# Two chunks' inner products in one visit of the matrix engine, and four copies of each sample token

## The chip, the core and the metric

The kernel runs on one core of a Trainium2 chip. The metric is the device time of one execution in microseconds: before the change 1611.52 us, the median of three runs (1607.17 to 1611.88 us). A core has the matrix engine TensorE (PE; its weight loads are listed as PEld), VectorE (DVE), ScalarE (ACT), GpSimd (POOL) and SyncE (SP), which here issues the transfers (DMAs). PE writes into PSUM, eight banks of 512 float32 numbers per partition. Each engine works through its own queue in order and waits at semaphores for the others.

## The reference

Two layers stand one behind the other in a residual trunk: a pooling mixer and a Mamba-2 state-space (SSD) mixer. They run over a prompt of 1024 tokens and over 8 sample sequences of 8 tokens with carried states. The part that matters here, cut to its core:

```python
# x: tokens x heads x 64;  B, C: tokens x groups x 128;  chunks of 128 tokens
a_cum = cumsum(dt * A, within the chunk)
L  = exp(where(causal, a_cum[i] - a_cum[j], -inf))
y_diag = einsum((C_i . B_j) * L[i, j] * dt[j], x[j])              # inside the chunk
state  = einsum(B[j], exp(a_cum[end] - a_cum[j]) * dt[j], x[j])   # what the chunk adds
h_next = exp(a_cum[end]) * h + state                              # from chunk to chunk
y_off  = einsum(C[i], h, exp(a_cum[i]))                           # from the incoming state
y = y_diag + y_off
```

The samples use the same formulas with chunks of 8 tokens. All is float32.

## The kernel before

Features lie on the partitions. The kernel works through two halves (h = 0, 1); each holds 512 prompt tokens and four sample sequences of 8 tokens (32 columns), so T = 544. Each projection is made by `product` (L166) in three float32r passes (high part by high, high by low, low by high), two halves of 272 columns each. `layer0` is the pooling mixer of one half, `layer1` the SSD mixer. The low parts of the SSD weights are made ahead by `stash` (L133 to L137), in buffers named L and bA, and stored.

`layer1` runs over four groups of heads; a group has two quads of four heads. `ssd` handles the prompt tokens of a quad, in four chunks of 128 tokens. For a chunk it loads the cumulated decays (bA), masks them on POOL (L624), takes the exponentials on ACT (L628) and multiplies by the C.B products on DVE (L629), which gives L. PE transposes x (L632), DVE scales it into xd and xs (L636). Four products xd by L (L639), each 64 columns of the array wide, go into the bank dg. The incoming state gives two products (L648) into the bank `of`, which DVE multiplies by the decays bE (L649) and to which it adds dg (L651). The product L655 gives what the chunk adds to the state; POOL decays the old state (L660) and DVE adds (L661). In half 0 the first chunk has no incoming state and its dg is copied by ACT (L653).

`ssd_sample` does the same for the 32 sample tokens of a quad. What they add to the state is made by one float32r product per sequence (L724) over 96 rows: three copies of each token (high part, low part and high part of B against high, high and low part of x).

The program's order is not written by hand: a scheduler lays out each engine's queue from the code and its priorities, so that the many large products L166 of projections stand between the small products of `ssd`. A change of buffers or of code order lays out all queues anew.

Of the kernel before, what the change touches and what calls it, by code (L numbers as in the profile page):

```python
# [9 lines left out]
F32 = mybir.dt.float32  # L10
F32R = mybir.dt.float32r
AF = mybir.ActivationFunctionType
ALU = mybir.AluOpType
# [3 lines left out]
P = 128  # L17
# [4 lines left out]
NH = 32  # L22
HD = 64
NS = 128
LP = 512
NB = 4
LS = 8
SM = NB * LS
# [9 lines left out]
Q = 128  # L38
NCH = LP // Q
# [6 lines left out]
C_ROW = C_SMASK + SM  # L46
# [16 lines left out]
def constants():  # L63
    c = np.zeros((P, C_END), np.float32)
    c[:, C_ID:C_ID + 128] = np.eye(128)
    j, i = np.meshgrid(np.arange(SM), np.arange(SM), indexing="ij")
    m = (j <= i) & (j // LS == i // LS)
    for r in range(3):
        c[r * SM:(r + 1) * SM, C_SMASK:C_SMASK + SM] = m
        for b in range(NB):  # L70
            c[r * SM + b * LS:r * SM + (b + 1) * LS, C_ROW + b] = 1.0
    c[:, C_INV:C_INV + 16] = np.float32(1.0) / np.arange(1, 17, dtype=np.float32)
    return c
# [3 lines left out]
def pool_ssd_step(ctx, tc, xin, spool, sconv, sssm, w_pin, w_mix, w_pout, w_sin, w_dt, w_sout, params, consts,  # L77
                  y_out, pool_p, pool_s, conv_p, conv_s, ssm_p, ssm_s):
    nc = tc.nc
    V, S, G, PE = nc.vector, nc.scalar, nc.gpsimd, nc.tensor  # L80
# [48 lines left out]

    def stash(n):  # L130
        for k, src, a, b in todo[:n]:
            raw = sp.tile([P, 512], F32, name="L", bufs=3)[:, :b - a]
            nc.sync.dma_start(out=raw, in_=src[:, a:b])  # L133
            hl = sp.tile([P, 512], F32R, name="bA", bufs=2)[:, :b - a]
            S.copy(hl, raw)  # L135
            V.tensor_tensor(out=hl, in0=raw, in1=hl, op=ALU.subtract)  # L136
            nc.sync.dma_start(out=low[k][:, a:b], in_=hl.bitcast(F32))  # L137
        del todo[:n]
# [324 lines left out]
    acd = [dp.tile([NCH, NH, Q], F32, name=f"acd{h}") for h in range(2)]  # L463
# [8 lines left out]
    def dt_part(h, act):  # L472
# [62 lines left out]
            nc.sync.dma_start(out=d2[:, k], in_=d1[h][k].rearrange("(b h) l -> h b l", b=NB))  # L535
        nc.sync.dma_start(out=asd[h], in_=d2[:, 0].rearrange("h b l -> h (b l)"))
        nc.sync.dma_start(out=esd[h], in_=d2[:, 3].rearrange("h b l -> h (b l)"))
        d3 = sp.tile([NH, 3, 3, SM], F32, name="cd")
        for k in range(3):
            G.tensor_copy(out=d3[:, k], in_=d2[:, k:k + 1].rearrange("h k b l -> h k (b l)").broadcast_to([NH, 3, SM]))  # L540
        sat = sp.tile([3 * SM, 3, NH], F32, name="sat")
        pt = sps.tile([P, 3, NH], F32, name="tr", bufs=2)
        for k in range(3):
            PE.transpose(pt[:3 * SM, k], d3[:, k].rearrange("p r s -> p (r s)"), ident[:NH, :NH])
        S.mul(sat[:, 0], pt[:3 * SM, 0], -1.0)
        S.copy(sat[:, 1:], pt[:3 * SM, 1:])
        return nat, sat, cdb

    def conv_part(h, act, g, j):
# [51 lines left out]
    def heads(x):  # L601
        return x.rearrange("p (e d) -> p e d", e=4)
# [4 lines left out]
    def by_head(x, i):  # L607

        return x[:, i:i + 4, None].broadcast_to([x.shape[0], 4, HD])

    def ssd(h, g, q, x, ys, C, com, nat, cdb):
        h0 = g * 8 + q * 4
        hf = None
        if h == 1:
            hf = sp.tile([P, 2 * P], F32, name=f"hf{q}", bufs=2)
            nc.sync.dma_start(out=hf, in_=hsd[g, q])
        for c in range(NCH):
            cs = slice(c * Q, (c + 1) * Q)
            ci = c * NH + h0
            bs, bt = com[c]  # L620

            bA = sp.tile([P, 4, Q], F32, name="bA", bufs=2)
            nc.sync.dma_start(out=bA, in_=acd[h][c:c + 1, h0:h0 + 4].broadcast_to([P, 4, Q]))
            G.affine_select(out=bA, in_=bA, pattern=[[0, 4], [1, Q]], compare_op=ALU.is_ge, fill=-1e30, base=0,  # L624
                            channel_multiplier=-1)
            L = sp.tile([P, 4, Q], F32, name="L", bufs=3)
            for e in range(4):
                S.activation(out=L[:, e], in_=bA[:, e], func=AF.Exp, bias=nat[:, 0, ci + e:ci + e + 1])  # L628
            V.tensor_tensor(out=L, in0=L, in1=bs.broadcast_to([P, 4, Q]), op=ALU.mult)  # L629
            px = sps.tile([P, 2 * P], F32, name="tr", bufs=2)  # L630
            for k in range(2):
                PE.transpose(px[:, k * P:(k + 1) * P], x[:, k, cs], ident)  # L632
            xd = sp.tile([P, 2 * P], F32, name="xd", bufs=2)
            xs = sp.tile([P, 2 * P], F32, name="xs", bufs=2)
            for k, x1 in enumerate((xd, xs)):
                V.tensor_tensor(out=heads(x1), in0=heads(px), in1=by_head(nat[:, 1 + k], ci), op=ALU.mult)  # L636
            pd = sps.tile([P, 2, Q], F32, name="dg")
            for e in range(4):
                PE.matmul(pd[e % 2 * HD:(e % 2 + 1) * HD, e // 2], xd[:, e * HD:(e + 1) * HD], L[:, e], start=True,  # L639
                          stop=True)  # L640
            if hf is not None:
                bE = sp.tile([P, 2, Q], F32, name="bE", bufs=2)
                ev = ecd[h][c:c + 1, h0:h0 + 4].rearrange("c (k r) i -> c r k i", r=2)
                for r in range(2):
                    nc.sync.dma_start(out=bE[r * 64:(r + 1) * 64], in_=ev[:, r].broadcast_to([64, 2, Q]))
                po = sps.tile([P, 2, Q], F32, name="of")
                for k in range(2):
                    PE.matmul(po[:, k], hf[:, k * P:(k + 1) * P], C[:, cs], start=True, stop=True)  # L648
                V.tensor_tensor(out=ys[:, :, cs], in0=po, in1=bE, op=ALU.mult)  # L649
            if hf is not None:  # L650
                V.tensor_tensor(out=ys[:, :, cs], in0=ys[:, :, cs], in1=pd, op=ALU.add)  # L651
            else:
                S.copy(ys[:, :, cs], pd)  # L653
            pst = sps.tile([P, 2 * P], F32, name="stt")
            PE.matmul(pst, bt, xs, start=True, stop=True)  # L655
            hn = sp.tile([P, 2 * P], F32, name=f"hf{q}", bufs=2)
            if hf is None:
                S.copy(hn, pst)
            else:
                G.tensor_tensor(out=heads(hn), in0=heads(hf), in1=by_head(cdb, ci), op=ALU.mult)  # L660
                V.tensor_tensor(out=hn, in0=hn, in1=pst, op=ALU.add)  # L661
            hf = hn
        nc.sync.dma_start(out=ssm_p[g, q] if h == 1 else hsd[g, q], in_=hf)

    K3 = 3 * SM

    def sample_common(B, C):
        ss = slice(LP, T)

        bd = sp.tile([P, 3, SM], F32R, name="bd")  # L670
        S.copy(bd[:, 0], B[:, ss])
        V.tensor_tensor(out=bd[:, 1], in0=B[:, ss], in1=bd[:, 0], op=ALU.subtract)
        S.copy(bd[:, 2], B[:, ss])
        pb = sps.tile([P, NS], F32R, name="tr", bufs=2)
        PE.transpose(pb[:K3], bd.rearrange("p r s -> p (r s)"), idr)
        Bm = sp.tile([K3, NB, NS], F32R, name="Bm")
        for b in range(NB):
            V.tensor_scalar(out=Bm[:, b], in0=pb[:K3], scalar1=cst[:K3, C_ROW + b:C_ROW + b + 1], scalar2=None,
                            op0=ALU.mult)
        pS = sps.tile([P, SM], F32, name="tr", bufs=2)  # L680
        PE.matmul(pS[:SM], B[:, ss], C[:, ss], start=True, stop=True)
        Sm = sp.tile([SM, 1, SM], F32, name="Ss")
        V.tensor_tensor(out=Sm[:, 0], in0=pS[:SM], in1=cst[:SM, C_SMASK:C_SMASK + SM], op=ALU.mult)
        return Bm, Sm

    def ssd_sample(h, g, q, x, ys, C, com, sat, cdb):
# [11 lines left out]
        xr = sp.tile([P, 2, 3, SM], F32, name="xr")  # L698
        V.tensor_copy(out=xr, in_=x[:, :, None, ss].broadcast_to([P, 2, 3, SM]))
        for k in range(2):  # L700
            PE.transpose(px[:K3, k * P:(k + 1) * P], xr[:, k].rearrange("p r s -> p (r s)"), ident)
# [3 lines left out]
        V.tensor_tensor(out=heads(xs[:K3]), in0=heads(px[:K3]), in1=by_head(sat[:, 2], h0), op=ALU.mult)  # L705
        xh = sp.tile([K3, 2 * P], F32R, name="xh", bufs=2)
        S.copy(xh, xs[:K3])
        r2 = slice(2 * SM, 3 * SM)
        V.tensor_tensor(out=xh[r2], in0=xs[r2], in1=xh[r2], op=ALU.subtract)
        pd = sps.tile([P, 2, SM], F32, name="dg")  # L710
        for e in range(4):
# [305 lines left out]
```

## Time and profile before

| what | us |
|---|---|
| median of three runs | 1611.52 |
| the profiled execution | 1614.12 |
| its span, first to last instruction | 1612.3 |
| PE busy (modelled), of the span | 1571.3 |
| DVE busy | 1086.4 |
| ACT busy | 740.6 |
| POOL busy | 325.7 |
| mean granted clock of PE, of full speed | 0.992 |

PE's records overlap: a product is recorded from its start until its result is out, so the distance between starts tells what it costs the queue. A float32 product is recorded as two matrix instructions, one of float32r as one. Busy shares are of the profiled execution, which lies 2.6 us above the median.

### The profile page before, as it was taken

To read this page: it belongs to the slowest core of one execution; us is meant where nothing else is said; L and a number is where in the kernel's file an instruction comes from. 1 tells how busy PE (TensorE), PEld (TensorE's weight loads), DVE (VectorE), ACT (ScalarE), POOL (GpSimd) and SP (SyncE) were. 2 spreads that over 40 slices of the span, in tenths; PEclk is the share of its full clock that TensorE was granted. 3 is DMA by queue.
4 is the path that set the end of the run, shared out by engine and by line. 5 is a ranking of instruction groups with operands and counts; after the bars stand their busy time and mean duration, and the time that the engine had idled before them with its cause. 6 is when DMAs were issued, how large, how long until landed. Compare 5 with 4: busy or idle time off the path is not lost.

```text
span 1612.3 us, 33214 instructions
## 1 busy us (share of the span) xinstructions
PE 1571.3 (97%) x12644; PEld 1515.7 (94%) x12644; DVE 1086.4 (67%) x2108; ACT 740.6 (46%) x1454; POOL 325.7 (20%) x536
## 2 busy tenths in 40 slices
PE   9989999999999999999999999999999999999996
PEld 8989999999999999999898999989988999999995
DVE  7787878875446475668575476667768765765666
ACT  5554444554232324265555454543634645535432
POOL 1200000003100010023413113222326432131213
PEclk9999999999999999999999999999999999999998
DMA  8878788886323234465756656665666666575662
GB/s 288 295 241 281 252 283 273 298 260 210 100 84 98 93 91 123 134 196 154 231 165 211 196 174 201 202 209 183 205 204 194 215 194 212 174 215 181 190 229 93
DMA packets 163407, 315.82 MB, mean 196 GB/s; under 512 B 33072, under 2 KB 71600, under 8 KB 163248
## 3 DMA queue, kind: packets, MB, share of 16 engines
q1 hardware_dynamic: 163248, 313.70, 61.1%
q8 instruction: 99, 1.62, 0.4%
q14 instruction: 60, 0.49, 0.1%
HBM read 262.47 MB, written 51.16 MB: 195 GB/s over the span
## 4 chain that ended last, share of the span: by engine, by line
PE 81%; DMA 8%; DVE 5%; ACT 2%; issue 2%; POOL 1%; SPq 0%; DVEq 0%; ACTq 0%; POOLq 0%
PE big L166 70%; DMA low<-bA 4%; PE dg L639 2%; PE stt L655 2%; PE of L648 2%; DMA bA<-acd 1%; DMA bAs<-asd 1%; PE tr L632 1%; DMA sq<-x2d 1%; DVE bA L136 1%; DMA L<-in_w_sin_dram 1%; PE big L386 1%; PE stt L724 1%; PE of L720 1%; DVE wlo L151 1%
## 5 line engine op out<-in xcount | busy, mean ns | idle before, releaser
L166 PE MATMUL big<-ah,whi 128*128 128x272 f32 (+1 forms) x2304 | 668.6, 290 | 4.1 <-DVE X L776 2.5
L166 PE MATMUL big<-al,whi 128*128 128x272 f32 (+1 forms) x2304 | 668.1, 290 | 0.0
L166 PE MATMUL big<-ah,wlo 128*128 128x272 f32 (+1 forms) x2304 | 666.8, 289 | 0.0
L166 PEld LDWEIGHTS big<-ah,whi 128*128 128x128 f32 (+1 forms) x2304 | 433.1, 188 | 7.9 <-DVE X L776 2.7
L166 PEld LDWEIGHTS big<-ah,wlo 128*128 128x128 f32 (+1 forms) x2304 | 433.5, 188 | 2.0 <-issue 1.1
L166 PEld LDWEIGHTS big<-al,whi 128*128 128x128 f32 (+1 forms) x2304 | 433.4, 188 | 1.4 <-issue 0.4
L166 PE MATMUL big<-y,whi 128*128 128x272 f32 x2048 | 405.1, 293 | 8.1 <-DVE z L747 3.3
L149 ACT CAST whi<-raw 128x1024 fp32r<-128x1024 f32 (+1 forms) x228 | 237.6, 1042 | 295.1 <-PE big L166 244.4
L166 PEld LDWEIGHTS big<-y,whi 128*128 128x128 f32 x2048 | 325.2, 189 | 13.7 <-DVE z L747 3.7
L166 PE MATMUL big<-y,wlo 128*128 128x272 f32 x1024 | 298.2, 291 | 0.0
L151 DVE TENSOR_TENSOR wlo<-raw,whi 128x1024 fp32r<-128x1024 f32 x112 | 139.2, 1243 | 107.6 <-ACT whi L149 105.7
L166 PEld LDWEIGHTS big<-y,wlo 128*128 128x128 f32 x1024 | 194.4, 190 | 0.9 <-issue 0.3
L565 DVE SCALAR_TENSOR_TENSOR win<-u,par,win 128x556 f32<-128x556 f32 x144 | 118.4, 823 | 46.6 <-ACT win L563 43.9
L628 ACT ACTIVATE L<-bA,nat 128x128 f32<-128x128 f32 x256 | 82.2, 392 | 83.0 <-PE dg L639 77.8
L135 ACT CAST bA<-L 128x512 fp32r<-128x512 f32 (+1 forms) x113 | 69.9, 619 | 95.4 <-DMA low<-bA 80.0
L136 DVE TENSOR_TENSOR bA<-L,bA 128x512 fp32r<-128x512 f32 (+1 forms) x113 | 78.9, 701 | 32.9 <-ACT bA L135 32.7
L166 PE MATMUL big<-p,whi 128*128 128x272 f32 x512 | 96.5, 288 | 0.0
L624 POOL TENSOR_SCALAR_AFFINE_SELECT bA<-bA 128x512 f32<-128x512 f32 x64 | 48.5, 759 | 162.6 <-DMA bA<-acd 136.0
L166 PEld LDWEIGHTS big<-p,whi 128*128 128x128 f32 x512 | 80.2, 188 | 0.0
L422 DVE TENSOR_TENSOR X<-X,big 128x272 f32<-128x272 f32 x128 | 54.7, 433 | 35.1 <-PE big L166 34.9
L726 POOL TENSOR_TENSOR ho<-hs,cdb 128x256 f32<-128x256 f32 x64 | 49.4, 778 | 138.4 <-DMA out_ssm_s_dram<-ho 79.5
L178 ACT COPY u<-big 128x272 f32<-128x272 f32 (+2 forms) x192 | 52.6, 308 | 50.9 <-PE big L166 34.4
(213 smaller groups left out, 1946.9 us busy)
## 6 DMA issues: line engine op xcount, KB each, us to landing
wlo<-low SPq DMA_DIRECT2D x114, 512.0 KB, 3.7
raw<-in_w_sin_dram SPq DMA_DIRECT2D x80, 512.0 KB, 4.9
raw<-in_w_pin_dram SPq DMA_DIRECT2D x64, 512.0 KB, 3.8
low<-bA SPq DMA_DIRECT2D x112, 256.0 KB, 4.0
L<-in_w_sin_dram SPq DMA_DIRECT2D x80, 256.0 KB, 4.3
raw<-in_w_sout_dram SPq DMA_DIRECT2D x34, 512.0 KB, 4.7
raw<-in_w_pout_dram SPq DMA_DIRECT2D x32, 512.0 KB, 4.0
bA<-acd SPq DMA_DIRECT2D x64, 256.0 KB, 4.2
```

Of the source, the lines that this page charges most:

```text
L135: S.copy(hl, raw)
L136: V.tensor_tensor(out=hl, in0=raw, in1=hl, op=ALU.subtract)
L149: S.copy(hi[:, :cols], raw[:, :cols])
L151: V.tensor_tensor(out=lo[:, :cols], in0=raw[:, :cols], in1=hi[:, :cols], op=ALU.subtract)
L166: PE.matmul(ps, w[:, wsl], x[:, cols], start=first, stop=kt == kts - 1 and a == 2)
L178: S.copy(out, ps)
L422: return lambda n, ps: V.tensor_tensor(out=half(X[d], n), in0=half(X[d], n), in1=ps, op=ALU.add)
L565: V.scalar_tensor_tensor(out=a[:, :n], in0=x[:, k:k + n], scalar=pcol(V_CW + ti * 4 + k), in1=a[:, :n], op0=ALU.mult, op1=ALU.add)
L624: G.affine_select(out=bA, in_=bA, pattern=[[0, 4], [1, Q]], compare_op=ALU.is_ge, fill=-1e30, base=0, channel_multiplier=-1)
L628: S.activation(out=L[:, e], in_=bA[:, e], func=AF.Exp, bias=nat[:, 0, ci + e:ci + e + 1])
L639: PE.matmul(pd[e % 2 * HD:(e % 2 + 1) * HD, e // 2], xd[:, e * HD:(e + 1) * HD], L[:, e], start=True, stop=True)
L726: G.tensor_tensor(out=heads(ho), in0=heads(hs), in1=by_head(cdb, (NCH + b) * NH + h0), op=ALU.mult)
```

## The change

Chunks are taken two at a time. For each of the two, the inputs of the inner product are made as before (L, xd, xs); then the eight products of both go into one bank dg of 512 columns (L645 now), next the state steps of both chunks, with the products of the incoming state in one bank `of` (L659) and the decays in one tile bE of twice the width, which has one buffer instead of two. One product and one sum on DVE then cover both chunks. L has four buffers instead of three, in `stash` as well. For the samples, each token has four copies instead of three: both parts of B against the high part of x twice and the low part twice, so 128 rows, the low by low term among them.

```diff
-            raw = sp.tile([P, 512], F32, name="L", bufs=3)[:, :b - a]
+            raw = sp.tile([P, 512], F32, name="L", bufs=4)[:, :b - a]
...
-        for c in range(NCH):
...
-            pd = sps.tile([P, 2, Q], F32, name="dg")
-            for e in range(4):
-                PE.matmul(pd[e % 2 * HD:(e % 2 + 1) * HD, e // 2], xd[:, e * HD:(e + 1) * HD], L[:, e], start=True,
-                          stop=True)
-            if hf is not None:
-                bE = sp.tile([P, 2, Q], F32, name="bE", bufs=2)
...
-                po = sps.tile([P, 2, Q], F32, name="of")
-                for k in range(2):
-                    PE.matmul(po[:, k], hf[:, k * P:(k + 1) * P], C[:, cs], start=True, stop=True)
-                V.tensor_tensor(out=ys[:, :, cs], in0=po, in1=bE, op=ALU.mult)
-            if hf is not None:
-                V.tensor_tensor(out=ys[:, :, cs], in0=ys[:, :, cs], in1=pd, op=ALU.add)
-            else:
-                S.copy(ys[:, :, cs], pd)
+        for c0 in range(0, NCH, 2):
+
+            pd = sps.tile([P, 2, 2 * Q], F32, name="dg")
+            xds, xss, Ls = [], [], []
+            for c in (c0, c0 + 1):
...
+                L = sp.tile([P, 4, Q], F32, name="L", bufs=4)
...
+            for n in range(2):
+                for e in range(4):
+                    PE.matmul(pd[e % 2 * HD:(e % 2 + 1) * HD, e // 2, n * Q:(n + 1) * Q], xds[n][:, e * HD:(e + 1) * HD],
+                              Ls[n][:, e], start=True, stop=True)
+            first = 1 if hf is None else 0
+            po = sps.tile([P, 2, 2 * Q], F32, name="of")
+            bE = sp.tile([P, 2, 2 * Q], F32, name="bE")
+            for n in range(2):
...
+                if hf is not None:
...
+                        nc.sync.dma_start(out=bE[r * 64:(r + 1) * 64, :, ns], in_=ev[:, r].broadcast_to([64, 2, Q]))
+                    for k in range(2):
+                        PE.matmul(po[:, k, ns], hf[:, k * P:(k + 1) * P], C[:, cs], start=True, stop=True)
+                pst = sps.tile([P, 2 * P], F32, name="stt")
+                PE.matmul(pst, com[c][1], xss[n], start=True, stop=True)
...
+            if first:
+                S.copy(ys[:, :, c0 * Q:(c0 + 1) * Q], pd[:, :, :Q])
+            fs = slice((c0 + first) * Q, (c0 + 2) * Q)
+            V.tensor_tensor(out=ys[:, :, fs], in0=po[:, :, first * Q:], in1=bE[:, :, first * Q:], op=ALU.mult)
+            V.tensor_tensor(out=ys[:, :, fs], in0=ys[:, :, fs], in1=pd[:, :, first * Q:], op=ALU.add)
...
-        bd = sp.tile([P, 3, SM], F32R, name="bd")
-        S.copy(bd[:, 0], B[:, ss])
-        V.tensor_tensor(out=bd[:, 1], in0=B[:, ss], in1=bd[:, 0], op=ALU.subtract)
-        S.copy(bd[:, 2], B[:, ss])
+        bd = sp.tile([P, 4, SM], F32R, name="bd")
+        for r in (0, 2):
+            S.copy(bd[:, r], B[:, ss])
+            V.tensor_tensor(out=bd[:, r + 1], in0=B[:, ss], in1=bd[:, r], op=ALU.subtract)
...
-        xh = sp.tile([K3, 2 * P], F32R, name="xh", bufs=2)
-        S.copy(xh, xs[:K3])
-        r2 = slice(2 * SM, 3 * SM)
+
+        xh = sp.tile([P, 2 * P], F32R, name="xh", bufs=2)
+        S.copy(xh, xs)
+        r2 = slice(2 * SM, 4 * SM)
         V.tensor_tensor(out=xh[r2], in0=xs[r2], in1=xh[r2], op=ALU.subtract)
```

How the scheduler's order moves is seen at two places. The first is PE's queue in half 0, group 1, second quad, chunks 2 and 3 (about 877 to 884 us of the trace). `dg<-L,xd` are the inner products, `of<-p,hf` those of the incoming state, `stt<-xs,bt` what the chunk adds to the state, `big` the large products; x4 stands for four instructions in a row. Before:

```order
L166 MATMUL big<-y_9852,whi 128x272 x2
L648 MATMUL of<-p_10046,hf_10743 128x128 x2
L639 MATMUL dg<-L,xd 64x128 x4
L655 MATMUL stt<-xs,bt 128x256
L166 MATMUL big<-y_9852,wlo 128x272
...
L166 MATMUL big<-y_9844,whi 128x272
L639 MATMUL dg<-L,xd 64x128 x4
L648 MATMUL of<-p_10046,hf_10779 128x128 x2
L655 MATMUL stt<-xs,bt 128x256
L166 MATMUL big<-y_9844,whi 128x272
```

And after, at the same place:

```order
L166 MATMUL big<-y_10269,whi 128x272 x2
L659 MATMUL of<-p_10035,hf_10723 128x128 x2
L645 MATMUL dg<-L,xd 64x128 x8
L661 MATMUL stt<-xs,bt 128x256
L166 MATMUL big<-y_10269,wlo 128x272
```

The second chunk's four inner products now stand right behind the first chunk's; the second chunk's other two rows (`of`, `stt`) keep their place further on.

The second place is SP's queue of transfers for the same quad: bA and bE as above, `wlo` and `raw` the parts of the large weights, `hsd` the state that half 0 leaves to half 1. Before:

```order
L623 DMA bA<-acd_143 128x512 x2
L645 DMA bE<-ecd_145 64x2x128 x2
L153 DMA wlo<-low_127 128x1024
L146 DMA raw<-in_w_sout_dram 128x1024
L645 DMA bE<-ecd_145 64x2x128 x2
L623 DMA bA<-acd_143 128x512
L645 DMA bE<-ecd_145 64x2x128
L663 DMA hsd<-hf_10460 128x256
```

After:

```order
L626 DMA bA<-acd_143 128x512 x2
L657 DMA bE<-ecd_145 64x2x128 x3
L153 DMA wlo<-low_127 128x1024
L657 DMA bE<-ecd_145 64x2x128
L146 DMA raw<-in_w_sout_dram 128x1024
L626 DMA bA<-acd_143 128x512 x2
L657 DMA bE<-ecd_145 64x2x128 x2
L674 DMA hsd<-hf_10442 128x256
```

The transfers into bE come in fours, one four for each pair that has two incoming states, with both bA of the next pair ahead of the second pair's bE.

## Rows read from the trace of the kernel before

**Rows 1.** The page: busy time of PE; the chain by engine.
```profile
PE 1571.3 (97%) x12644; PEld 1515.7 (94%) x12644; DVE 1086.4 (67%) x2108; ACT 740.6 (46%) x1454; POOL 325.7 (20%) x536
...
PE 81%; DMA 8%; DVE 5%; ACT 2%; issue 2%; POOL 1%; SPq 0%; DVEq 0%; ACTq 0%; POOLq 0%
```
**Rows 2.** Stretches: length; busy us (instructions) by engine; clock, DMA share, GB/s.
```profile
30.00:700.00 670.00, 661.43 (x5253) 658.32 (x5252) 458.68 (x791) 286.01 (x451) 54.95 (x84) 0.99 0.62 196
700.00:1560.00 860.00, 845.90 (x6839) 799.52 (x6838) 572.15 (x1218) 420.38 (x942) 250.25 (x423) 0.99 0.62 197
```
**Rows 3.** Timeline of PE around one visit: start us, us, instruction.
```profile
849.07 0.29 PE L166 MATMUL big<-al,whi 128*128 128x272 f32 x1
849.29 0.66 PE L639 MATMUL dg<-L,xd 128*64 128x128 f32 x8
849.88 0.39 PE L166 MATMUL big<-ah,wlo 128*128 128x272 f32 x1
850.11 0.29 PE L166 MATMUL big<-ah,whi 128*128 128x272 f32 x1
```
**Rows 4.** The same visit in two narrow windows of the timeline.
```profile
849.29 0.33 PE L639 MATMUL dg<-L,xd 128*64 128x128 f32 x2
...
849.45 0.50 PE L639 MATMUL dg<-L,xd 128*64 128x128 f32 x6
```
**Rows 5.** Instructions of tile dg: ns min/median/max, first and last start.
```profile
L639 PE MATMUL dg<-L,xd x512: 272/273/476, 727.9 to 1545.8; 128*64 128x128 f32 x171
...
L651 DVE TENSOR_TENSOR ys<-ys,dg x56: 399/415/423, 736.1 to 1547.6; 128x256 f32<-128x256 f32 x56
L740 DVE TENSOR_TENSOR ys<-ys,dg x16: 201/214/222, 752.9 to 1554.8; 128x64 f32<-128x64 f32 x16
```
**Rows 6.** Chain in order of time: start us, us, what.
```profile
851.64 0.44 PE of L648 x4
...
882.01 0.59 PE dg L639 x8
882.60 0.64 PE of L648 x4
```
**Rows 7.** Timeline of PE around one sample product of 96 rows.
```profile
862.65 0.28 PE L166 MATMUL big<-y,wlo 128*128 128x272 f32 x1
862.77 0.29 PE L724 MATMUL stt<-xh,Bm 96*128 96x256 f32 x1
862.89 0.41 PE L166 MATMUL big<-y,whi 128*128 128x272 f32 x2
```
**Rows 8.** What PE waited for: us in total, times, longest us.
```profile
PE big L166 <- DVE X L776: 5.2, 4, 2.5
PE big L166 <- DVE z L747: 3.3, 2, 2.8
...
PE of L648 <- DVE hf L661: 1.8, 2, 1.2
```
**Rows 9.** Stretches behind the longest of these waits.
```profile
1083.00:1086.00 3.00, 2.08 (x18) 1.43 (x16) 0.00 (x0) 0.00 (x0) 0.30 (x1) 1.00 1.03 396
1086.00:1089.00 3.00, 1.13 (x5) 1.13 (x6) 2.28 (x5) 1.50 (x4) 0.89 (x2) 0.68 0.68 265
1089.00:1092.00 3.00, 3.00 (x16) 2.75 (x17) 3.00 (x7) 2.26 (x6) 0.61 (x1) 0.50 0.33 99
1092.00:1095.00 3.00, 3.00 (x22) 2.67 (x19) 2.85 (x6) 0.46 (x1) 0.00 (x0) 0.68 0.33 94
```
**Rows 10.** Tile bE: its reader on DVE, and its transfers.
```profile
L649 DVE TENSOR_TENSOR ys<-of,bE x56: 402/424/427, 734.5 to 1546.7; 128x256 f32<-128x256 f32 x56
...
DMA to landing us min/median/max: 2.5/3.2/7.9
```
**Rows 11.** Line L135 on ACT: its instructions, and its longest wait.
```profile
L135 ACT CAST bA<-L x113: 401/621/633, 15.8 to 361.8; 128x512 fp32r<-128x512 f32 x112, 128x256 fp32r<-128x256 f32 x1
...
  DMA low<-bA: 80.0, 75
```

More of the change, by code (lines that the diff above doesn't have):

```diff
@@ L67, in constants @@
     m = (j <= i) & (j // LS == i // LS)
-    for r in range(3):
+    for r in range(P // SM):
         c[r * SM:(r + 1) * SM, C_SMASK:C_SMASK + SM] = m
@@ L537, in dt_part @@
         nc.sync.dma_start(out=esd[h], in_=d2[:, 3].rearrange("h b l -> h (b l)"))
-        d3 = sp.tile([NH, 3, 3, SM], F32, name="cd")
+        d3 = sp.tile([NH, 3, 4, SM], F32, name="cd")
         for k in range(3):
-            G.tensor_copy(out=d3[:, k], in_=d2[:, k:k + 1].rearrange("h k b l -> h k (b l)").broadcast_to([NH, 3, SM]))
-        sat = sp.tile([3 * SM, 3, NH], F32, name="sat")
+            G.tensor_copy(out=d3[:, k], in_=d2[:, k:k + 1].rearrange("h k b l -> h k (b l)").broadcast_to([NH, 4, SM]))
+        sat = sp.tile([P, 3, NH], F32, name="sat")
         pt = sps.tile([P, 3, NH], F32, name="tr", bufs=2)
         for k in range(3):
-            PE.transpose(pt[:3 * SM, k], d3[:, k].rearrange("p r s -> p (r s)"), ident[:NH, :NH])
-        S.mul(sat[:, 0], pt[:3 * SM, 0], -1.0)
-        S.copy(sat[:, 1:], pt[:3 * SM, 1:])
+            PE.transpose(pt[:, k], d3[:, k].rearrange("p r s -> p (r s)"), ident[:NH, :NH])
+        S.mul(sat[:, 0], pt[:, 0], -1.0)
+        S.copy(sat[:, 1:], pt[:, 1:])
         return nat, sat, cdb
@@ L616, in ssd @@
             nc.sync.dma_start(out=hf, in_=hsd[g, q])
-        for c in range(NCH):
[L618 to L626, printed above, removed]
-            for e in range(4):
-                S.activation(out=L[:, e], in_=bA[:, e], func=AF.Exp, bias=nat[:, 0, ci + e:ci + e + 1])
-            V.tensor_tensor(out=L, in0=L, in1=bs.broadcast_to([P, 4, Q]), op=ALU.mult)
-            px = sps.tile([P, 2 * P], F32, name="tr", bufs=2)
-            for k in range(2):
[L632 to L636, printed above, removed]
-            pd = sps.tile([P, 2, Q], F32, name="dg")
-            for e in range(4):
-                PE.matmul(pd[e % 2 * HD:(e % 2 + 1) * HD, e // 2], xd[:, e * HD:(e + 1) * HD], L[:, e], start=True,
-                          stop=True)
-            if hf is not None:
-                bE = sp.tile([P, 2, Q], F32, name="bE", bufs=2)
-                ev = ecd[h][c:c + 1, h0:h0 + 4].rearrange("c (k r) i -> c r k i", r=2)
-                for r in range(2):
-                    nc.sync.dma_start(out=bE[r * 64:(r + 1) * 64], in_=ev[:, r].broadcast_to([64, 2, Q]))
-                po = sps.tile([P, 2, Q], F32, name="of")
-                for k in range(2):
-                    PE.matmul(po[:, k], hf[:, k * P:(k + 1) * P], C[:, cs], start=True, stop=True)
-                V.tensor_tensor(out=ys[:, :, cs], in0=po, in1=bE, op=ALU.mult)
-            if hf is not None:
-                V.tensor_tensor(out=ys[:, :, cs], in0=ys[:, :, cs], in1=pd, op=ALU.add)
-            else:
-                S.copy(ys[:, :, cs], pd)
[L654 to L662, printed above, removed]
@@ new lines, in ssd @@
+        for c0 in range(0, NCH, 2):
+            pd = sps.tile([P, 2, 2 * Q], F32, name="dg")
+            xds, xss, Ls = [], [], []
+            for c in (c0, c0 + 1):
+                cs = slice(c * Q, (c + 1) * Q)
+                ci = c * NH + h0
+                bA = sp.tile([P, 4, Q], F32, name="bA", bufs=2)
+                nc.sync.dma_start(out=bA, in_=acd[h][c:c + 1, h0:h0 + 4].broadcast_to([P, 4, Q]))
+                G.affine_select(out=bA, in_=bA, pattern=[[0, 4], [1, Q]], compare_op=ALU.is_ge, fill=-1e30, base=0,
+                                channel_multiplier=-1)
+                L = sp.tile([P, 4, Q], F32, name="L", bufs=4)
+                for e in range(4):
+                    S.activation(out=L[:, e], in_=bA[:, e], func=AF.Exp, bias=nat[:, 0, ci + e:ci + e + 1])
+                V.tensor_tensor(out=L, in0=L, in1=com[c][0].broadcast_to([P, 4, Q]), op=ALU.mult)
+                px = sps.tile([P, 2 * P], F32, name="tr", bufs=2)
+                for k in range(2):
+                    PE.transpose(px[:, k * P:(k + 1) * P], x[:, k, cs], ident)
+                xd = sp.tile([P, 2 * P], F32, name="xd", bufs=2)
+                xs = sp.tile([P, 2 * P], F32, name="xs", bufs=2)
+                for k, x1 in enumerate((xd, xs)):
+                    V.tensor_tensor(out=heads(x1), in0=heads(px), in1=by_head(nat[:, 1 + k], ci), op=ALU.mult)
+                xds.append(xd)
+                xss.append(xs)
+                Ls.append(L)
+            for n in range(2):
+                for e in range(4):
+                    PE.matmul(pd[e % 2 * HD:(e % 2 + 1) * HD, e // 2, n * Q:(n + 1) * Q], xds[n][:, e * HD:(e + 1) * HD],
[4 more added lines that the diff above has]
+            for n in range(2):
+                c = c0 + n
+                cs = slice(c * Q, (c + 1) * Q)
+                ns = slice(n * Q, (n + 1) * Q)
+                if hf is not None:
+                    ev = ecd[h][c:c + 1, h0:h0 + 4].rearrange("c (k r) i -> c r k i", r=2)
+                    for r in range(2):
+                        nc.sync.dma_start(out=bE[r * 64:(r + 1) * 64, :, ns], in_=ev[:, r].broadcast_to([64, 2, Q]))
[3 more added lines that the diff above has]
+                PE.matmul(pst, com[c][1], xss[n], start=True, stop=True)
+                hn = sp.tile([P, 2 * P], F32, name=f"hf{q}", bufs=2)
+                if hf is None:
+                    S.copy(hn, pst)
+                else:
+                    G.tensor_tensor(out=heads(hn), in0=heads(hf), in1=by_head(cdb, c * NH + h0), op=ALU.mult)
+                    V.tensor_tensor(out=hn, in0=hn, in1=pst, op=ALU.add)
+                hf = hn
+            if first:
[3 more added lines that the diff above has]
+            V.tensor_tensor(out=ys[:, :, fs], in0=ys[:, :, fs], in1=pd[:, :, first * Q:], op=ALU.add)
@@ L663, in ssd @@
         nc.sync.dma_start(out=ssm_p[g, q] if h == 1 else hsd[g, q], in_=hf)
-    K3 = 3 * SM
     def sample_common(B, C):
         ss = slice(LP, T)
-        bd = sp.tile([P, 3, SM], F32R, name="bd")
-        S.copy(bd[:, 0], B[:, ss])
-        V.tensor_tensor(out=bd[:, 1], in0=B[:, ss], in1=bd[:, 0], op=ALU.subtract)
-        S.copy(bd[:, 2], B[:, ss])
+        bd = sp.tile([P, 4, SM], F32R, name="bd")
+        for r in (0, 2):
+            S.copy(bd[:, r], B[:, ss])
+            V.tensor_tensor(out=bd[:, r + 1], in0=B[:, ss], in1=bd[:, r], op=ALU.subtract)
@@ L674, in sample_common @@
         pb = sps.tile([P, NS], F32R, name="tr", bufs=2)
-        PE.transpose(pb[:K3], bd.rearrange("p r s -> p (r s)"), idr)
-        Bm = sp.tile([K3, NB, NS], F32R, name="Bm")
+        PE.transpose(pb, bd.rearrange("p r s -> p (r s)"), idr)
+        Bm = sp.tile([P, NB, NS], F32R, name="Bm")
         for b in range(NB):
-            V.tensor_scalar(out=Bm[:, b], in0=pb[:K3], scalar1=cst[:K3, C_ROW + b:C_ROW + b + 1], scalar2=None,
-                            op0=ALU.mult)
+            V.tensor_scalar(out=Bm[:, b], in0=pb, scalar1=cst[:, C_ROW + b:C_ROW + b + 1], scalar2=None, op0=ALU.mult)
@@ L697, in ssd_sample @@
         px = sps.tile([P, 2 * P], F32, name="tr", bufs=2)
-        xr = sp.tile([P, 2, 3, SM], F32, name="xr")
-        V.tensor_copy(out=xr, in_=x[:, :, None, ss].broadcast_to([P, 2, 3, SM]))
+        xr = sp.tile([P, 2, 4, SM], F32, name="xr")
+        V.tensor_copy(out=xr, in_=x[:, :, None, ss].broadcast_to([P, 2, 4, SM]))
         for k in range(2):
-            PE.transpose(px[:K3, k * P:(k + 1) * P], xr[:, k].rearrange("p r s -> p (r s)"), ident)
+            PE.transpose(px[:, k * P:(k + 1) * P], xr[:, k].rearrange("p r s -> p (r s)"), ident)
         xd = sp.tile([P, 2 * P], F32, name="xd", bufs=2)
@@ L704, in ssd_sample @@
         V.tensor_tensor(out=heads(xd[:SM]), in0=heads(px[:SM]), in1=by_head(sat[:SM, 1], h0), op=ALU.mult)
-        V.tensor_tensor(out=heads(xs[:K3]), in0=heads(px[:K3]), in1=by_head(sat[:, 2], h0), op=ALU.mult)
-        xh = sp.tile([K3, 2 * P], F32R, name="xh", bufs=2)
-        S.copy(xh, xs[:K3])
-        r2 = slice(2 * SM, 3 * SM)
+        V.tensor_tensor(out=heads(xs), in0=heads(px), in1=by_head(sat[:, 2], h0), op=ALU.mult)
+        xh = sp.tile([P, 2 * P], F32R, name="xh", bufs=2)
+        S.copy(xh, xs)
+        r2 = slice(2 * SM, 4 * SM)
         V.tensor_tensor(out=xh[r2], in0=xs[r2], in1=xh[r2], op=ALU.subtract)
```

## The prediction

> **What bounds the kernel now.** I read the busy shares and the chain first, then the engines by stretch, then the matrix engine's timeline, then what it waits for. The page gives PE as busy for 97% of the span and the chain puts 81% on it [rows 1]. Cut by stretch, PE is modelled busy for 845.90 of the 860 us between 700 and 1560 us, which is the whole state-space layer that the change touches; DVE is busy for 572.15 us there and ACT for 420.38 us [rows 2]. So in this stretch about 14 us are PE waiting, and the rest is PE at work: what shortens the end is fewer microseconds of PE's own sequence, or fewer of those 14 us. The granted clock is 0.99 there, so nearly all of it runs at 2.4 GHz.
>
> A busy PE need not be a PE that streams. The timeline shows where it does not. Products of the large projections (L166, 272 columns) start 0.12 to 0.13 us apart [rows 7]; this is their slot. Around one visit of the products inside a chunk (L639, four products, recorded as eight) the starts are not in step [rows 3]: the last large one before it starts at 849.07, the first small one at 849.29 instead of about 849.20, the next large one at 849.88, and the one after that only at 850.11, 0.23 us later. From 849.07 to 850.11 are 1.04 us; less the two slots of the large products, 0.79 us are what the visit costs.
>
> Inside the visit the products go in pairs, one to each half of the array's columns (the row's form says 128*64). The first pair starts at 849.29; six records from 849.45 on take 0.50 us [rows 4], and one record is 0.27 us long [rows 5], so three pairs start over 0.23 us, 0.115 us a pair. Four pairs at that pace are 0.46 us. The other 0.33 us is the price of coming and going: 0.09 us on entry, 0.045 us between first and second pair, 0.20 us on leaving. The leaving part is seen apart in the chain: the four records of L648 take 0.44 us after large products and 0.64 us straight after a visit [rows 6]. It is paid whatever follows.
>
> The Trainium skill's page "TensorEngine Tiling (Array Packing)", section "Key Properties", says that a change of tiling mode drains the engine; the 0.33 us agree for the 64-column form, and the page has no price of its own.
>
> **The change, part by part.** *Joined visits.* The order of PE's instructions shows it at second quads: before, the small products of two chunks stand 15 rows apart with one 128*128 product after another between them; now eight stand in one row. Counted over the whole order, the small products make 66 separate visits before (64 groups of four, two of them cut in two) and 37 after: 27 groups of eight and ten of four, since five pairs are cut by a few other products. So 29 visits go, and no column or product goes with them: the trace has 512 records of L639 [rows 5], and after will have as many. 29 x 0.33 us = 9.6 us, all on PE, all in the stretch where PE is the bound. Bounds: if the second four products bring their own start-up, a join leaves 0.59 us for them [rows 6] instead of 0.46, and saves 0.79 - 0.59 = 0.20 us, 5.8 us in all; above 0.33 us there is nothing left to save, because the pair pace is array time. Zero or a loss would need PE to wait for the second chunk, which is the slower rival below. I take 0.33 us because the pairs in the middle of a visit are the nearest thing to a fifth pair.
>
> *One product and one sum for two chunks (L649, L651).* 24 pairs lose two DVE instructions each (in the first half of the sequence the first chunk has no incoming state, so its pair keeps its short forms). A 256-column one is 0.415 us, a 64-column one 0.214 us [rows 5], so 1.05 ns a column and 0.68 us for 512 columns, against 0.83 us for two: 48 x 0.15 us = 7 us off DVE. DVE is busy for two thirds of the stretch, and PE waits for it in places only; I count nothing. The bounds are zero and the waits of PE in that stretch; a microsecond or two would be my guess if any of it shows.
>
> *One buffer of twice the width for bE.* The same 112 transfers, 3.2 us to landing [rows 10]. The second pair's transfers now wait in SP's queue until DVE has read the first pair's, and behind them in the queue stand the next mask input bA, the states' transfers and weights. Before, the second buffer was freed by every other chunk. Among PE's releasers there is no DMA, and a unit of weights is consumed in 48 slots, 6.0 us, with three buffers; a hold of a few microseconds on SP is covered by that. If the cover is gone, it is the hold itself that shows. I count nothing.
>
> *A fourth buffer L.* It also serves the stage up to 362 us in which weights are split and their low parts stored. There the cast on ACT (L135) waits for the store of bA, 80.0 us in 75 waits [rows 11], and bA keeps its two buffers. A deeper L lets a load start earlier that then waits for the same store. PE is idle for 8.6 us of the 670 us from 30 us on, before the layer [rows 2], so this can give or take a few microseconds at most; I count nothing.
>
> *Four copies of each token.* The sample product L724 goes from 96 rows to 128 and the transposes to 128 wide. In the trace such a product stands between two large ones with 0.12 us to either side [rows 7]: a plain slot, with nothing of the 0.33 us. So it costs nothing now and frees nothing. The two transposes (128 moving columns already) keep their time. DVE gets one more subtraction of 32 columns a group, eight in all at about 0.2 us, beside PE.
>
> By the rule on modes in the Trainium skill's page "TensorEngine Tiling (Array Packing)", section "Key Properties", a drain of its own would stand around each of these products if 96 rows were a mode; the trace has none there, and the case is the last rival.
>
> **The sum.** The profiled execution took 1614.1 us, 1612.3 of it span; minus 9.6 it would be 1604.5. It lies 2.6 us above the median of the three runs, 1611.5, to which the same difference is applied: 1611.5 - 9.6 = 1602.
>
> **Rivals.** *The second four bring their own start-up.* 0.20 us a join: 1611.5 - 5.8 = 1605.7. For it: the first pair's step of 0.16 us is longer than the others, and the operands come from another chunk's tiles. Against: each pair in a visit has its own weights already, and they keep 0.115 us.
>
> *The order that comes with it makes new waits.* All queues are laid out anew, and waits depend on where a late transfer meets an in-order queue. The longest now is PE waiting 2.8 us for DVE's L747 [rows 8], in the windows from 1083 us on; behind it the granted clock falls to 0.50 and recovers, so that 12 us hold 61 products [rows 9] where 96 slots fit: some 4.4 us for one such event. Two more of them are 8.8 us and the gain is gone: about 1611. For it: both kinds of wait sit in queues whose order changes. Against: the layer has two such waits over 2 us in 860 us (the other is for L776, 2.5 us [rows 8]), and the change may as well remove one as add one.
>
> *A pair waits for its later chunk; slower.* One mechanism, at the 16 second pairs: their first state product L648 writes the bank that DVE frees only when it has multiplied both chunks' results by bE, and that product waits for the first pair's second state, which comes through POOL (L660) and DVE (L661). The trace has this wait twice, 1.2 us the longer [rows 8]. At every second pair it would be 16 x 1.2 = 19 us: 1621. It eats the gain from 0.6 us a pair, and is measurably slower from 0.9 us. For it: the bank that was freed chunk by chunk is now freed by twos. Against: in the new order some 24 large products, 3.0 us, stand between a chunk's state product and the next L648, as before, and the shortest gap, some 11 of them with a joined visit, is 2.7 us, while L649 lasts 0.42 us [rows 10] and L651, much like L661 in shape, 0.415 us [rows 5].
>
> *96 rows empty the array too.* If PE treats a product of 96 rows as another form and empties itself around it, 128 rows save up to 0.33 us at each of the 64 products beside the joins: 1602 - 21 = 1581. For it: after a visit of another form the product does start late. Against: between large products it does not [rows 7].
>
> **How the numbers follow.** Forecast as summed, near 1602: 0.59. Own start-up: 0.12. New waits: 0.21. Slower: 0.06. 96 rows: 0.02. A measurement of this kernel tells about 0.3%, 4.8 us, from no change, so faster is below 1606.7 and slower above 1616.3. Faster: 0.59 + 0.12 + 0.02 = 0.73; same 0.21; slower 0.06. The likeliest case alone spans 1597 to 1607 (two of the waits in the layer gone, or one event more). The range reaches from 1594, where also the event behind rows 9 is gone (4.4 us) and some of DVE's 7 us shows, to 1611, where the gain is eaten; the slower case is left out.
>
> **What would show it.** Right: the new line of L639 has 512 records in about 37 visits, a visit of sixteen records lasts about 1.05 us from its first start to the next product's start, and the product after that shows its 0.10 us once; PE's modelled idle time in the layer stays near 14 us. Own start-up: a gap of some 0.16 us in the middle of each visit. New waits: PE rows with DVE or POOL as releasers whose sum is over 20 us in the layer, or another stretch at 0.50 clock. Slower: L648 waiting for DVE at sixteen places. Sample product: its neighbours still at 0.12 us. The prediction is wrong if the visits are joined and cost 0.59 us per four all the same, or if the layer does not get shorter by 6 to 12 us.

## The result and the profile after

The changed kernel takes 1600.88 us (median of ten runs, 1593.97 to 1605.2), the kernel before 1612.53 us in ten runs beside it: a ratio of 0.992 [0.9901, 0.994], 11.65 us less. The forecast was 1602, between 1594 and 1611. The profiled execution took 1600.0 us, 1598.2 of it span, against 1614.1 and 1612.3.

The page of the changed kernel, as in [rows 1]:

```profile
PE 1557.1 (97%) x12644; PEld 1512.8 (95%) x12644; DVE 1084.2 (68%) x2068; ACT 735.7 (46%) x1454; POOL 323.7 (20%) x536
...
PE 76%; DMA 11%; DVE 7%; ACT 3%; issue 2%; POOL 1%; SPq 0%; DVEq 0%; ACTq 0%; POOLq 0%
```

PE has as many instructions as before and is busy for 14.2 us less; DVE has 40 fewer and is busy for only 2.2 us less. To see where the end moved, I cut both executions at two places that both have: the first start of L433 (the loads of X that open the second part of the program) and the last start of the sum into X (L776, now L785). Tile X of the kernel before:

```profile
L776 DVE TENSOR_TENSOR X<-X,big x94: 378/430/440, 964.5 to 1589.8; 128x272 f32<-128x272 f32 x94
...
L433 SPq DMA_DIRECT2D X<-in_xin_dram x8: 328/333/382, 371.8 to 395.5; - x8
```

and of the changed one:

```profile
L785 DVE TENSOR_TENSOR X<-X,big x94: 415/429/440, 963.5 to 1575.6; 128x272 f32<-128x272 f32 x94
...
L433 SPq DMA_DIRECT2D X<-in_xin_dram x8: 328/333/382, 376.9 to 400.4; - x8
```

Between them the stretch (columns as in [rows 2]) was in the kernel before

```profile
371.80:1589.80 1218.00, 1201.36 (x9696) 1152.76 (x9699) 773.95 (x1552) 545.08 (x1144) 292.68 (x478) 1.00 0.55 174
```

and is in the changed one, with the stretches of [rows 2] and two others behind it,

```profile
376.90:1575.60 1198.70, 1185.82 (x9694) 1148.78 (x9696) 771.26 (x1511) 540.79 (x1145) 292.44 (x478) 1.00 0.56 177
...
30.00:700.00 670.00, 657.75 (x5215) 654.40 (x5214) 455.90 (x784) 282.11 (x443) 51.51 (x80) 0.99 0.61 194
700.00:1560.00 860.00, 848.81 (x6988) 813.32 (x6988) 581.72 (x1206) 427.13 (x961) 252.85 (x428) 1.00 0.64 202
...
1086.00:1089.00 3.00, 3.00 (x26) 2.95 (x24) 3.00 (x7) 1.08 (x2) 0.07 (x1) 1.00 0.72 193
...
1224.00:1227.00 3.00, 0.77 (x3) 0.72 (x4) 3.00 (x6) 0.00 (x0) 1.83 (x2) 0.52 0.55 202
1227.00:1230.00 3.00, 3.00 (x15) 3.00 (x15) 2.96 (x8) 1.13 (x3) 1.44 (x3) 0.50 0.54 150
```

So the pair of executions differs by -14.1 us in span like this: the stage ahead took 5.1 us longer (376.9 against 371.8), the cut stretch 19.3 us less, the tail the same (22.6 against 22.5). Of the 19.3 us, 15.5 are PE's busy time and 3.8 its waiting (16.64 to 12.88 us). The stretch at half clock of [rows 9] is gone: PE is full at 1.00 from 1086 us on. The other such stretch of the layer, from 1230 us on in the kernel before (0.57 granted from 1230 to 1233 us), has its counterpart from 1224 us on, inside and behind the longest wait of the layer. What PE waits for now, as in [rows 8]:

```profile
PE big L166 <- DVE u L180: 5.9, 3, 2.5
PE stt L733 <- DVE ho L736: 4.2, 1, 4.2
...
PE big L166 <- DVE X L785: 2.5, 2, 1.7
PE of L659 <- DVE hf L667: 1.8, 1, 1.8
```

The wait for z is no longer among them. The sample products waited for ho three times before, 1.2 us at the longest,

```profile
PE stt L724 <- DVE ho L727: 2.3, 3, 1.2
```

and now wait once, for 4.2 us. The first state product of a pair (L659) waits once, not sixteen times. PE's 512 records of the inner products stand in 37 visits, 27 of sixteen records and ten of eight. The visit itself, in PE's timeline, and below it a sample product (now 128 rows):

```profile
848.85 0.60 PE L661 MATMUL stt<-xs,bt 128*128 128x256 f32 x2
849.38 1.09 PE L645 MATMUL dg<-L,xd 128*64 128x128 f32 x16
850.40 0.44 PE L635 MATMUL tr<-cst,p 128*128 128x128 f32 x2
...
857.31 0.28 PE L733 MATMUL stt<-xh,Bm 128*128 128x256 f32 x1
857.43 0.41 PE L166 MATMUL big<-y,whi 128*128 128x272 f32 x2
```

Sixteen records last 1.02 us from their first start to the next product's (1.05 forecast), where two visits of eight took 0.59 us each [rows 6]: 0.16 us less in the visit alone, and one leaving less behind it. The sample product keeps its 0.12 us. The chain shows the leaving part once for each joined visit: two transposes after it take 0.37 us, 0.22 elsewhere:

```profile
839.54 0.22 PE tr L635 x2
...
844.33 0.44 PE of L659 x4
...
849.45 1.02 PE dg L645 x16
850.47 0.37 PE tr L635 x2
```

Tile dg, as in [rows 5]:

```profile
L645 PE MATMUL dg<-L,xd x512: 272/273/324, 738.3 to 1530.0; 128*64 128x128 f32 x171
...
L673 DVE TENSOR_TENSOR ys<-ys,dg x32: 405/677/687, 747.9 to 1535.8; 128x512 f32<-128x512 f32 x24, 128x256 f32<-128x256 f32 x8
```

The sum over 512 columns takes 0.677 us; 0.68 was forecast.

### The profile page after: what moved, and what is told of

Same layout as the page of the kernel before. It is cut to its first block, busy times and chain, and to the rows that moved or that the text cites. A ratio compares the mean times of both kernels' runs of the same rounds, so it can differ in the third digit from the quotient of the medians.

```text
span 1598.2 us, 33156 instructions
## 1 busy us (share of the span) xinstructions
PE 1557.1 (97%) x12644; PEld 1512.8 (95%) x12644; DVE 1084.2 (68%) x2068; ACT 735.7 (46%) x1454; POOL 323.7 (20%) x536
## 4 chain that ended last, share of the span: by engine, by line
PE 76%; DMA 11%; DVE 7%; ACT 3%; issue 2%; POOL 1%; SPq 0%; DVEq 0%; ACTq 0%; POOLq 0%
PE big L166 66%; DMA low<-bA 8%; PE dg L645 2%; PE stt L661 2%; DVE bA L136 2%; PE of L659 1%; ACT bA L135 1%; PE tr L635 1%; DMA out_ssm_s_dram<-ho 1%; DVE win L565 1%; DVE X L852 1%; PE big L386 1%; DVE wlo L151 1%; PE stt L733 1%; PE of L729 1%
## 5 line engine op out<-in xcount | busy, mean ns | idle before, releaser
L166 PE MATMUL big<-y,whi 128*128 128x272 f32 x2048 | 400.8, 292 | 7.6 <-DVE X L785 2.5
L135 ACT CAST bA<-L 128x512 fp32r<-128x512 f32 (+1 forms) x113 | 69.7, 619 | 97.0 <-DMA low<-bA 80.6
L166 PE MATMUL big<-p,wlo 128*128 128x272 f32 x256 | 73.6, 288 | 0.0
```

The costliest lines, as they stand in the source:

```text
L166: PE.matmul(ps, w[:, wsl], x[:, cols], start=first, stop=kt == kts - 1 and a == 2)
```

## The experiments

The theory: what counts is how often PE changes to the 64-column form, about 0.33 us there and back, whichever product follows. Against it: DVE's joined operations, the four copies, the buffers, or the new order with its waits. The ratios are to the kernel before, timed beside each.

**The visits apart again, the rest as changed** (`e1`, 65 visits).

```
-            for c in (c0, c0 + 1):
+            def ready(c):          # makes the operands of one chunk
...
-                xd = sp.tile([P, 2 * P], F32, name="xd", bufs=2)
+                xd = sp.tile([P, 2 * P], F32, name="xd")
...
-            for n in range(2):
+            def inner(n):          # the four products of one chunk
...
+                ready(c)           # both called in the loop of the state steps
+                inner(n)
```

> The changed kernel with its banks, bE and one DVE product and sum for two chunks, but the inner products of the two chunks apart again: each chunk's inputs are made just before its own products, and xd has one buffer instead of two, so the second four cannot stand beside the first (65 visits instead of 37). Theory (the visits are what is saved): 28 visits come back at 0.33 us, +9 us against the changed kernel, so 1608 to 1613 where before has 1612; a visit of eight records lasts 0.59 us again. Rival (the shorter DVE work, the wider banks or the new order save the time): it stays within 3 us of the changed kernel, 1599 to 1604.

Measured: 1618.52 us, 1.0024 [1.001, 1.0037]. The gain is gone, with the joined banks, the wide DVE operations, the one bE and the four copies still there. It came out 4.3 us slower than the kernel before beside it (1614.2), outside of what was expected, and why is not shown: the edit also leaves xd one buffer instead of two and puts the second chunk's preparation behind the first one's state step. This run alone therefore doesn't separate the visits from these two; the dose below, which leaves both alone, does. The cut stretch, as above:

```profile
377.40:1591.80 1214.40, 1199.34 (x9697) 1152.05 (x9700) 765.40 (x1512) 544.52 (x1145) 313.93 (x478) 1.00 0.55 175
```

PE is busy in it about as long as in the kernel before.

**DVE's two operations apart again** (`e2`, 37 visits).

```
-            V.tensor_tensor(out=ys[:, :, fs], in0=po[:, :, first * Q:], ...)   # both chunks
+            for n in range(first, 2):                                          # each by itself
+                V.tensor_tensor(out=ys[:, :, fs], in0=po[:, :, ns], ...)
```

> The changed kernel with the joined visits, but one DVE product and one sum for each chunk instead of one for both. Theory: DVE gets 7 us of work back that lies beside PE, so 0 to +2 us against the changed kernel: 1600 to 1604, with 37 visits. Rival (DVE's work decides): +7 us, near 1608.

Measured: 1598.34 us, 0.9902 [0.9884, 0.992]: not slower than the changed kernel, and a little under the expected range. The sum is 56 operations again:

```profile
L675 DVE TENSOR_TENSOR ys<-ys,dg x56: 403/414/422, 744.5 to 1531.4; 128x256 f32<-128x256 f32 x56
```

What the wide form saves on DVE is worth nothing at the end. It doesn't show in DVE's busy time either: over the cut stretch that is 767.72 us here and 771.26 us in the changed kernel.

**Joined visits with three copies** (`e3`, 37 visits) and **four copies with the chunks one by one** (`e4`, 66 visits).

```
e3, against the changed kernel:  -    for r in range(P // SM):   +    for r in range(3):
e4, against the kernel before:   -    for r in range(3):         +    for r in range(P // SM):
```

and the tiles of the samples' states with 96 or 128 rows to match.

> The changed kernel with three copies of each sample token as before (products of 96 rows), everything else as changed. Theory: the copies are worth nothing, so within 2 us of the changed kernel: 1599 to 1604. Rival (products of 96 rows empty the array, or start their neighbours late): a good part of the gain is lost, 1606 to 1612.

> The kernel before with four copies of each sample token, nothing else. Theory: no change, 1609 to 1615 where before has 1612. Rival (96 rows cost something): 2 to 10 us below before.

Measured: 1604.52 us, 0.9942 [0.9929, 0.9955], and 1613.06 us, 0.9989 [0.9978, 1.0001]. The changed kernel without the fourth copy keeps most of the gain (its median lies 0.5 us above the expected range, on a chip where the kernel before took 1614.2 us); the copies alone can't be told from nothing, and the intervals of the changed kernel with three copies and with four overlap.

**The dose** (`e5`, `e6`). Three more products of 4 columns go into each pair's visit, in places that the real products overwrite later: in `e5` as one of 128 columns of the array, so that PE must change its form three more times, in `e6` as two halves in the form of the visit.

```
+    if e == 1 or (e == 3 and n == 0):
+        nk, nn = (1, n) if e == 1 else (0, 1)
+        PE.matmul(pd[:, nk, nn * Q:nn * Q + 4], ident, ident[:, :4], ...)                        # e5
+        for r in range(2):                                                                       # e6
+            PE.matmul(pd[r * HD:(r + 1) * HD, nk, nn * Q:nn * Q + 4], ident[:, r * HD:(r + 1) * HD], ident[:, :4], ...)
```

> The changed kernel with three short extra products in each pair's visit (4 moving columns, 128*128 form, into columns that the visit's next products overwrite), so that every visit is left and entered again three times: 96 more changes of form there and back. Theory (a change there and back costs 0.33 us whatever causes it): +32 us, and with the extra products' own time (0.05 to 0.11 us each, 5 to 10 us) 1637 to 1645 where the changed kernel has 1601; against the next run, which has the same products in the visit's own form, +25 to +32 us. Rival (what a visit costs is its first weights or the queue around it, not the form): about the same as the next run.

> The same three extra products per visit, each as two halves in the 128*64 form of the visit, so no form changes. Theory: only their own time, 96 times 0.05 to 0.11 us, +5 to +11 us against the changed kernel: 1606 to 1612. Rival (not the form): as the run with the 128*128 form.

Measured: 1637.6 us, 1.0153 [1.0132, 1.0173], and 1611.82 us, 0.9991 [0.9978, 1.0005]: 25.8 us between them. One visit of `e5` in PE's timeline:

```profile
845.18 0.44 PE L645 MATMUL dg<-L,xd 128*64 128x128 f32 x4
845.55 0.39 PE L649 MATMUL dg<-cst 128*128 128x4 f32 x2
845.87 0.44 PE L645 MATMUL dg<-L,xd 128*64 128x128 f32 x4
846.24 0.38 PE L649 MATMUL dg<-cst 128*128 128x4 f32 x2
```

and of `e6`:

```profile
850.54 0.42 PE L645 MATMUL dg<-L,xd 128*64 128x128 f32 x4
850.78 0.23 PE L650 MATMUL dg<-cst 128*64 128x4 f32 x4
850.87 0.42 PE L645 MATMUL dg<-L,xd 128*64 128x128 f32 x4
```

From one group of real products to the next it is 0.69 us (845.18 to 845.87) with a change of form between and 0.33 us (850.54 to 850.87) without: 0.36 us a change, with whatever the extra products' own times differ by. Over the cut stretch, `e5` first:

```profile
377.00:1613.70 1236.70, 1229.21 (x9877) 1173.96 (x9880) 762.74 (x1512) 545.14 (x1143) 293.34 (x478) 1.00 0.54 172
375.50:1585.60 1210.10, 1198.22 (x10064) 1161.23 (x10067) 763.20 (x1511) 542.04 (x1143) 298.02 (x478) 1.00 0.56 175
```

`e6` has 32 visits, not 37: with the extra products its order keeps all 32 pairs whole, 28 records each. So PE is busy for 31.0 us longer in `e5` for the 98 visits that it has more (130 against 32): 0.32 us each. The medians show 25.8 us of these 31.0; in the profiles `e5`'s PE also waits less there (7.5 us against 11.9), so that the stretch is 26.6 us longer.

**Three L buffers** (`e7`), and **the sample products C.B in the full form** (`e8`, built on `e2`).

```
e7  -  ... name="L", bufs=4)        (both places)
e7  +  ... name="L", bufs=3)
e8  -  PE.matmul(pS[:SM], B[:, ss], C[:, ss], start=True, stop=True)
e8  +  PE.matmul(pS, xpair[1].rearrange("p a t -> p (a t)")[:, LP:LP + P], C[:, ss], start=True, stop=True)
```

> The changed kernel with three buffers L instead of four, in the layer and in the stage that stores low parts. Theory: a fourth L gives the first stage nothing (it waits for stores of bA), and in the layer a pair's two L leave one to fill: within 3 us of the changed kernel, 1598 to 1604, still 37 visits. Rival (the fourth buffer is what pays): 1606 to 1612.

> The changed kernel with one DVE product and sum per chunk (as in the second experiment, 1598 there) and the samples' C.B product made 128 columns wide (its weights take 96 columns beyond the 32 that count, whose rows nobody reads), so that it needs no form of 32 columns: 8 more visits gone. Theory: 8 times about 0.3 us, 2.4 us below the second experiment, near 1596 where before has 1614. Rival: the order's own waits move by as much as that, and it cannot be told from the second experiment.

Measured: 1593.23 us, 0.9889 [0.9868, 0.9909], and 1597.65 us, 0.990 [0.9881, 0.992]. `e8` can't be told from `e2`: the eight 32-column visits that it has fewer would be some 2.6 us at 0.33 us, less than these intervals tell. `e7` came out 5 us below what was expected of it, which put the fourth buffer, so far counted at nothing, under suspicion. The last four runs, on one chip, went to that.

**The fourth L buffer alone, the changed kernel again, three buffers again, and three buffers with `e2`'s operations** (`e9` to `e12`; `e9` is the kernel before with `bufs=4` in both places).

> The kernel before with a fourth L buffer in both places and nothing else (66 visits, three copies). If the fourth buffer itself costs waits, as the gain of about 8 us from taking it out of the changed kernel suggests: 1616 to 1622. If what that gain showed is only how one order of the instructions falls out against another: within 4 us of the kernel before, either way.

> The changed kernel, timed beside the one with three L buffers on one chip. If the difference of the two (1600.9 against 1593.2, measured apart) is of the kernels: 5 to 10 us between their medians here again. If it was of the chips or the runs: under 3 us.

> The changed kernel with three L buffers, on the same chip as the changed kernel: 1591 to 1597 if its gain is its own, 1598 to 1602 if it was of the chips or the runs.

> Three L buffers and VectorE's two operations of a pair made for each chunk by itself (37 visits). If both small gains seen are mechanisms that add: 1588 to 1593. If each only shuffles the same waits: within 4 us of the changed kernel with three L buffers, 1590 to 1600.

Measured: 1613.24 us, 1.0004 [0.9992, 1.0015]; 1600.61 us, 0.9921 [0.9903, 0.994]; 1594.59 us, 0.9897 [0.9883, 0.991]; 1591.15 us, 0.9881 [0.9865, 0.9898]. The theory that a fourth buffer costs waits by itself falls: alone it does nothing. In the changed kernel the 6 us came again, though the two intervals just overlap, and so do single executions: 1593.64 to 1602.57 us with four buffers (`e10`), 1593.7 to 1597.51 with three (`e11`). Where the 6 us are isn't shown, because one profile each can't show it: the changed kernel's second profile is 5.3 us shorter than its first.

```profile
0.00:373.30 373.30, 359.66 (x2860) 354.77 (x2861) 300.20 (x525) 189.91 (x297) 30.68 (x57) 0.99 0.83 271
373.30:1570.40 1197.10, 1186.65 (x9698) 1149.02 (x9700) 773.33 (x1512) 542.09 (x1145) 291.49 (x478) 1.00 0.56 177
```

Same program, 3.6 us less ahead of the cut and 1.6 us less in it. `e12` is the fastest measured and faster than the kernel before, but its interval overlaps those of `e11` and `e2`, and its median fits both of the cases that were set against each other.

The cut over all kernels but the two of the dose, from one profile each:

| kernel | visits | ahead of the cut | cut stretch | PE busy in it | PE waiting |
|---|---|---|---|---|---|
| before | 66 | 371.8 | 1218.0 | 1201.36 | 16.6 |
| `e4` | 66 | 377.6 | 1213.6 | 1197.47 | 16.1 |
| `e9` | 66 | 380.8 | 1214.0 | 1200.89 | 13.1 |
| `e1` | 65 | 377.4 | 1214.4 | 1199.34 | 15.1 |
| changed | 37 | 376.9 | 1198.7 | 1185.82 | 12.9 |
| `e10`, the same | 37 | 373.3 | 1197.1 | 1186.65 | 10.4 |
| `e2` | 37 | 373.3 | 1200.4 | 1189.21 | 11.2 |
| `e3` | 37 | 380.6 | 1201.6 | 1188.12 | 13.5 |
| `e7`, `e11` | 37 | 371.3, 372.4 | 1197.1, 1200.8 | 1186.99, 1190.30 | 10.1, 10.5 |
| `e8` | 38 | 375.1 | 1199.4 | 1187.46 | 11.9 |
| `e12` | 37 | 380.9 | 1191.4 | 1183.60 | 7.8 |

PE's busy time there falls in two groups that don't touch: 1197.47 to 1201.36 us with 65 or 66 visits, 1183.60 to 1190.30 with 37 or 38 (in `e8` a sample product cuts one more pair). Within a group, copies, DVE's form and buffers make no order. The stage ahead of it takes 371 to 381 us in kernels of either group.

## Why the prediction was right

*Joined visits, 29 x 0.33 = 9.6 us.* Right in kind and nearly in size. `e1` takes the joins back and loses everything; the dose gives 0.32 us a change over the stretch and 0.36 us in a single visit. The three profiles with 66 visits have a mean of 1199.9 us of busy PE in the cut, the eight with 37 or 38 have 1187.3: 12.6 us, 3 us more than the term. Busy time also counts the stretches at half clock, which differ between profiles. Two visits of another form, that of the 32-column products L720, had been cut in two in the order before and are whole in the new one (18 to 16), which the count had left out. A sum that leaves both waits and clock out adds up the times from one PE start to the next over the whole trace, and puts a step that holds a wait or lies in a stretch of lower clock at the median of like steps. It gives 1559.5 us for the kernel before, 1559.8 for `e4`, 1557.9 for `e1`, and 1548.7 for the changed one: 9.2 us for the 28 visits between the last two, 0.33 each, and some 2 us that `e1` has gained as well, of which the L720 products make 1.1 (10.2 to 9.1). What the rest of these 2 us is stays open. By the same sum all kernels with 66 visits lie between 1559.5 and 1560.0 us, all with 37 or 38 between 1547.6 and 1549.4, and `e5` (1594.2) lies 33.1 us above `e6` (1561.1), 0.34 us a visit.

*The second four's own start-up* (the first rival, 1605.7): not there. The sixteen records go through in 1.02 us, less than the 1.05 forecast.

*DVE's wide operations, counted as nothing.* Right: their length was as worked out, and `e2` without them is no slower. The 7 us that they were to take off DVE can't be found in its busy time, which fell by 2.2 us over the span.

*One buffer for bE, counted as nothing.* No wait for it appears among PE's releasers; it wasn't tried by itself.

*The fourth L buffer, counted as nothing, a few microseconds at most either way.* The size was off, at or beyond the bound: 6 us between medians in the changed kernel (`e10`, `e11`), to the slower side. Its reason was not found, and `e9` shows that it is not the buffer alone.

*Four copies, counted as nothing.* Right: `e4`, and the 0.12 us slots. The last rival, that 96 rows empty the array, would have made `e4` some 21 us faster; its ratio is 0.9989.

*New waits* (1611) and *the pair that waits for its later chunk* (1621): neither came. PE waits 11.2 us in the stretch of 860 us, where it had waited 14.1, and L659 waits once. The one wait of 4.2 us for ho and the lost one of 2.8 us for z are the kind of exchange that the rival named; in this profile the event of [rows 9] went, and 5.1 us ahead of the layer came instead.

*How near the figure came* is in part luck. By the sums of starts PE's own work fell by 10.8 us, 1 us more than the joins were counted for. Between the means of the table, PE also waits 4 us less with the visits joined (11.0 against 15.3), for which no cause was shown. Against this, the version with four L buffers is 6 us slower than the one with three, whose medians (1593.23 and 1594.59 us) lie at the lower end of the forecast range, one of them outside it. The last sign that the prediction gave, a layer shorter by 6 to 12 us, holds for the medians, 11.65 us apart, but not for the profiles: there the cut stretch, which holds the layer, is 19.3 us shorter, and 20.9 us in the second profile of the changed kernel.

## What to carry to other kernels

Count how often the matrix engine changes between a full-width form and a half-width one, not the products of either: each there-and-back cost a third of a microsecond here, with operands ready and no wait in any list. Bringing two such visits together is worth that much where the engine is the bound, and merging the operations of an engine that is not the bound along with it was worth nothing that these runs could tell. Before explaining a few microseconds from two profiles, take a second profile of the same kernel.

## What the runs showed of the hardware that was not expected

- A change of form there and back costs about the same for a 4-column product as for a run of real ones: 0.36 us in the visit of `e5` and 0.32 us on the mean of the 98 visits that it has more than `e6`, beside 0.33 us for a joined visit.
- The stage ahead of the cut, in which weights are split and stored, varies from 371.3 to 380.9 us between profiled executions, and by 3.6 us between two of the same program; that is as much as most of the edits here were worth.
- With the wait of 4.2 us (L733, to 1226 us) the granted clock went to 0.50, 1.2 GHz, and behind it 15 products ran in the 3 us from 1227 us on, where 26 ran at 1.00 from 1086 us.
